# Who issues the loads: compression pages on SyncE alone, pair weights on Pool's queue half a pair ahead

## The chip, the cores and the metric

One core of a Trainium2 chip runs the whole program. The metric is the device time of one execution in microseconds; the median of several runs is compared. Traces are one profiled execution each, and times in them count from its first instruction.

## The reference

One layer of a decoder for a prompt of 1024 rows and 8 samples of 4 new rows each, 1056 rows in all, everything float32. What the change touches:

```
h = RMSNorm(x) * (1 + scale1) + shift1
z = h @ w_in          # columns: gMLP u|v, q, k/v of three branches, branch gates, merge gates
...
kv_rows = past rows from cache_kv[page_table] (8192 per sample) + the new ones
kc, vc  = compress_blocks(kv_rows)    # each 64-row block: gelu(einsum(block + pe, w1) + b1) @ w2 + b2
o_cmp, o_sel, o_win = attention over compressed blocks, over the top 16 blocks, over a window of 512
```

The compression reads the compressed-branch half of every page of all eight samples. Those pages are 64 MB of the traffic.

## The kernel before, in words

Products run with weights and activations split into two float32r parts each (hi and lo, three matmuls per product). `split` and `parts_into` make such parts: a cast on ScalarE (L332, L822) and a subtraction on VectorE (L333, L823).

The instructions are given to a scheduler, which makes an order for each engine in advance from the order of the program and from the times that it reckons with; on the chip each engine runs its own list strictly in order. A wait at the head of a list holds up all that stands behind it, and that goes for SyncE, ScalarE and Pool as issuers of DMAs too. In the attention stage the order on TensorE is that of the program. The DMAs of SyncE and ScalarE share eight completion semaphores in turn, so a DMA of the two waits until the one eight places before it has landed; Pool's DMAs have eight of their own.

The pages of the compressed branch come in 16 loads of 32 pages of 128 KB, one buffer. `step(n)` runs the compression of load n on TensorE (`compress`, 64 pairs of matmuls that each read all 32 pages), its activation on ScalarE (`compress_act`, L569), and then issues load n + 1 (`compress_load`). `load_pages` (L538) deals the eight groups of four pages out to queues: groups whose place modulo eight is in `share` go to ScalarE's queue, here (1, 4), the rest to SyncE's. Before each group the queue's engine reads four entries of the page table (L528).

The stages up to the attention: row products for keys and values (steps 1, 2), the gMLP stage (steps 3, 4), and then the pair stage. It computes columns of z two blocks at a time in 11 pairs (queries 2, merge gates 8, keys 1) with a scheme that saves one of eight quarter products. `pair` loads four raw weight tiles of 256 KB, a11, a12, a21, a22, into a ring of four buffers. It needs weight sums made on Pool, s1 = a21 + a22 and s2 = s1 - a11, later s3 = a11 - a21 (over a21) and s4 = a12 - s2 (over a12), and sums of parts of h (T2, T3, T4 and the changed B12). A quarter product is 12 matmuls of 304 columns; a11, a12, a21 and a22 are used on the remaining 448 columns as well. The order of weights in an ordinary pair is a11, a12, s2, a21, s3, s1, a22, s4. There are three buffers each for hi and lo parts, so a split can run up to three weights ahead of TensorE.

The sums of h are made once, in the opening pair: `sums_of(k)` for T2, T3 and T4, then `last_sums` for B12, on Pool, VectorE and ScalarE. The temporary `e` of `sums_of` lives in the tiles that later hold s1 and s2, so these come after the sums. `pair` is a generator; between its parts the loop runs `step(5)` to `step(14)`.

The attention follows. It has four page buffers (`page_buffer`), which hold window rows (w_k, w_v), selected pages (`psel`) and weights w_ada in turn. The first use of each buffer makes Pool copy one element of the loaded queries into its first element (L1064), so that what is loaded there waits for the queries.

Of the kernel before, what the change touches and what calls it, by code (L numbers as in the profile page):

```python
# [6 lines left out]
F32 = mybir.dt.float32  # L7
# [4 lines left out]
OP = mybir.AluOpType  # L12
# [7 lines left out]
HQ = 304  # L20
# [33 lines left out]
def step_kernel(tc, A):  # L54
    nc = tc.nc
    sync, act, dve, pool, pe = nc.sync, nc.scalar, nc.vector, nc.gpsimd, nc.tensor
# [19 lines left out]
    def new_pool(name, side=None):  # L76
        kw = {} if side is None else {"side": side}
        return TP(tc.alloc_tile_pool(name=name, bufs=1, reuse_waits="tile", **kw))
# [95 lines left out]
    for gr in range(2):  # L174
        e = tmpi([128, 32])
# [4 lines left out]
    for b in range(8):  # L180
        e = tmpi([128, 32], F32, "e", 2)
# [22 lines left out]
    e = tmpi([128, 32])  # L204
# [3 lines left out]
    W = new_pool("weights", "right")  # L208
# [121 lines left out]
    def split(t, hi, lo):  # L330

        act.copy(hi, t)  # L332
        dve.tensor_tensor(lo, t, hi.bitcast(F32), op=OP.subtract)  # L333
# [212 lines left out]
    def compress_load(n):  # L546
        b, half = n // 2, n % 2
        home = "a"
        st = PG([128, 32, 256], F32, "st", 1)
        load_pages([(st[:, i], A["pcmp"], b * 64 + half * 32 + i) for i in range(32)], freed.get(home),  # L550
                   (1, 4))
        paged[n] = st, home

    def compress(n):
# [120 lines left out]
    for tt in range(9):  # L675
        n = 128 if tt < 8 else 32
        st = RV2([128, 6], F32, "bn", 2)[0:n]
# [5 lines left out]
    for tt in range(9):  # L683
        n = 128 if tt < 8 else 32
# [43 lines left out]
    W = new_pool("weights2", "right")  # L728
# [85 lines left out]
    def out_tile():  # L814
        homes[0] += 1
        return TR([128, R], F32, "o", 1) if homes[0] % 3 == 0 else slot()

    def sum_tile(i):
        return TR([128, 512], F32, f"sum{i}", 1)

    def parts_into(x, hi, lo):
        act.copy(hi, x)  # L822
        dve.tensor_tensor(lo, x, hi.bitcast(F32), op=OP.subtract)  # L823

    def sums_of(k):

        (h11, l11), (h12, l12), (h21, l21), (h22, l22) = (f32(x[k]) for x in (B11, B12, B21, B22))
        t = TR([128, R], F32, "o", 1)
        f0, f1, d = (t[:, HQ * i:HQ * i + HQ] for i in range(3))
        e = sum_tile(k % 2)[:, 0:HQ]  # L830
        pool.tensor_tensor(d, l22, l12, op=OP.subtract)
        dve.tensor_tensor(f0, h22, h12, op=OP.subtract)
        dve.tensor_tensor(f0, f0, d, op=OP.add)
        dve.tensor_tensor(f1, f0, h11, op=OP.add)
        dve.tensor_tensor(f1, f1, l11, op=OP.add)
        parts_into(f1, *T2[k])
        pool.tensor_tensor(e, h21, f1, op=OP.subtract)
        pool.tensor_tensor(e, e, l21, op=OP.add)
        parts_into(f0, *T3[k])
        parts_into(e, *T4[k])  # L840
# [12 lines left out]
    def weight_parts(x):  # L853
        hi, lo = (W([128, 512], F32R, tag, 3) for tag in ("hi", "lo"))
        split(x, hi, lo)
        return [[t[:, c:c + 128] for c in range(0, 512, 128)] for t in (hi, lo)]
# [8 lines left out]

    rest = [tuple(t[:, 2 * HQ:R] for t in (hh[k], hl[k])) for k in range(8)]

    def pair(m, n, ev, opening=False, closing=False):

        raws = []  # L870
        for j, c in ((m, 0), (m, 512), (n, 0), (n, 512)):
            raws.append(W([128, 512], F32, "raw", 4))
            act.dma_start(raws[-1], A["w_t"][j][:, c:c + 512])
        a11, a12, a21, a22 = raws
        g, t = out_tile(), out_tile()
        first, second, third = slice(0, HQ), slice(HQ, 2 * HQ), slice(2 * HQ, R)
        plain = [pA()[:, 0:R - 2 * HQ] for _ in range(2)]
        X, S, Z = pA()[:, 0:HQ], pT()[:, 0:HQ], pT()[:, 0:HQ]
        add = lambda o, x, y: dve.tensor_tensor(o, x, y, op=OP.add)  # L879
        s1, s2 = sum_tile(0), sum_tile(1)  # L880

        w = weight_parts(a11)
        quarter_products(w, rest[0:4], plain[0], True, False)
        quarter_products(w, B11, X, True, True)
        act.copy(g[:, first], X)
        w = weight_parts(a12)
        quarter_products(w, rest[4:8], plain[0], False, True)
        quarter_products(w, B21, X, False, True)
        ev(t[:, third], plain[0])
        ev(t[:, first], X)  # L890
        yield
        pool.tensor_tensor(s1, a21, a22, op=OP.add)  # L892
        pool.tensor_tensor(s2, s1, a11, op=OP.subtract)
        if opening or closing:
            quarter_products(weight_parts(a21), rest[0:4], plain[1], True, False)
        if opening:
            quarter_products(weight_parts(a22), rest[4:8], plain[1], False, True)
            ev(g[:, third], plain[1])
            yield
        if not (opening or closing):  # L900
            quarter_products(weight_parts(s2), T2, S, True, True)
            add(t[:, second], S, g[:, first])
            quarter_products(weight_parts(a21), rest[0:4], plain[1], True, False)
        s3, s4 = a21, a12
        pool.tensor_tensor(s3, a11, a21, op=OP.subtract)
        pool.tensor_tensor(s4, a12, s2, op=OP.subtract)
        if closing:
            w = weight_parts(a22)
            quarter_products(w, rest[4:8], plain[1], False, True)
            ev(g[:, third], plain[1])  # L910
            Y = pA()[:, 0:HQ]
            quarter_products(w, T4, Y, True, True)
            quarter_products(weight_parts(s1), B12, Z, True, True)
            ev(g[:, second], Z)
            quarter_products(weight_parts(s4), B22, Z, False, True)
            ev(t[:, second], Z)
            w = weight_parts(s2), weight_parts(s3)
            quarter_products(w[0], T2, S, True, True)
            for o in (t, g):
                add(o[:, second], g[:, first], o[:, second])  # L920
            add(t[:, second], S, t[:, second])
            quarter_products(w[1], T3, S, False, True)
            add(g[:, first], Y, g[:, first])
            add(g[:, second], S, g[:, second])
            add(g[:, first], S, g[:, first])
            yield t, g
            return
        if opening:
            quarter_products(weight_parts(s2), T2, S, True, True)
            add(t[:, second], S, g[:, first])  # L930
        quarter_products(weight_parts(s3), T3, S, False, True)
        add(g[:, second], S, g[:, first])
        quarter_products(weight_parts(s1), B12, Z, True, True)
        add(g[:, second], Z, g[:, second])
        w = weight_parts(a22)
        quarter_products(w, T4, S, False, True)
        add(g[:, first], S, g[:, first])
        ev(g[:, 0:2 * HQ], g[:, 0:2 * HQ])
        if not opening:
            quarter_products(w, rest[4:8], plain[1], False, True)  # L940
            ev(g[:, third], plain[1])
        quarter_products(weight_parts(s4), B22, Z, False, True)
        add(t[:, second], Z, t[:, second])
        ev(t[:, second], t[:, second])
        yield t, g
# [29 lines left out]
                pool.dma_start(A["o_wsk"][b][:, 508:512], kr[:, NP + 4 * b:NP + 4 * b + 4])  # L975

    n = 5
    for i in range(11):
        j = 2 * i
        m, fn, ev, base = ((4 + j, query, scaled, 4) if i < 2 else (6 + j, merge_gate, gate, 10) if i < 10 else  # L980
                           (8, key, lambda o, x: act.copy(o, x), 8))
        work = pair(m, m + 1, ev, i == 0) if i < 10 else pair(9, 8, ev, False, True)
        next(work)
        if i == 0:
            for k in range(4):
                sums_of(k)
            next(work)
            last_sums()
        if i < 10:
            step(n)  # L990
            n += 1
        out = next(work)
        for x, j in zip(out, (m - base, m + 1 - base)) if i < 10 else zip(out[::-1], range(2)):
            fn(j, x)
        if i in (5, 6, 7, 8):
            next(first_blocks, None)
    for b in range(8):
# [44 lines left out]
    qt = [slot() for _ in range(4)]  # L1042
# [14 lines left out]
    def page_buffer():  # L1057

        n = len(uses)
        uses.append(None)  # L1060
        assert n < 4 or uses[n - 4] is not None
        st = R3S([128, 4, 4, 256], F32, f"st{n % 4}", 1)
        if n < 4:
            pool.tensor_copy(st[0:1, 0, 0, 0:1], qt[3][0:1, 0:1])  # L1064
        return n, st, uses[n - 4] if n >= 4 else None

    YS = R3([128, 8, 32])
# [373 lines left out]
    begin, m = None, 0  # L1441
# [124 lines left out]
    W = new_pool("weights3", "right")  # L1566
# [30 lines left out]
    for m in range(8):  # L1597
        t = slot()
# [56 lines left out]
    for a, b in CH:  # L1655
        acc = None
        for m in range(8):
            products(weights(A["w_out"][m], 8), mh, ml, a, b,
                     lambda a, b, ps, m=m: residual(x1[m], m, gate1, a, b, ps, x1[m]),
# [433 lines left out]
```

## Time and profile before

| what | value |
|---|---|
| median of 3 runs | 1952.53 us (1951.09 to 1954.44) |
| the profiled execution | 1954.05 us, span 1952.5 us |
| TensorE matmul busy | 1843.3 us, 94% of the span |
| TensorE weight load busy | 1707.8 us, 87% |
| VectorE, ScalarE, Pool busy | 1247.9, 837.7, 612.7 us |
| mean granted TensorE clock | 0.983 |
| HBM traffic | 178 GB/s over the span |

How to read it: PE is TensorE's matmuls and PEld its weight loads. DVE is VectorE, ACT ScalarE, POOL Pool (GpSimd) and SP SyncE; a q behind an engine's name means its sequencer, which waits and issues DMAs and isn't counted as busy. A row of the timeline gives start, duration, engine, line, operation, tiles, count, and in brackets the idle time before it with what ended it. Matmuls are pipelined and their ends are modelled.

### The profile page before, as it was taken

To read this page: it belongs to the slowest core of one execution; us is meant where nothing else is said; L and a number is where in the kernel's file an instruction comes from. 1 tells how busy PE (TensorE), PEld (TensorE's weight loads), DVE (VectorE), ACT (ScalarE), POOL (GpSimd) and SP (SyncE) were. 2 spreads that over 40 slices of the span, in tenths; PEclk is the share of its full clock that TensorE was granted. 3 is DMA by queue.
4 is the path that set the end of the run, shared out by engine and by line. 5 is a ranking of instruction groups with operands and counts; after the bars stand their busy time and mean duration, and the time that the engine had idled before them with its cause. 6 is when DMAs were issued, how large, how long until landed. Compare 5 with 4: busy or idle time off the path is not lost.

```text
span 1952.5 us, 43825 instructions
## 1 busy us (share of the span) xinstructions
PE 1843.3 (94%) x15905; PEld 1707.8 (87%) x15905; DVE 1247.9 (64%) x2547; ACT 837.7 (43%) x1707; POOL 612.7 (31%) x809
## 2 busy tenths in 40 slices
PE   5999969999998799999999999999999999999997
PEld 3999968989888577776779999899999999999997
DVE  7525264243426576776664768999988888756464
ACT  4413022222224464656661355644444444555343
POOL 2410242121213122222210511387766765301010
PEclk9999989999999899999999999999999999999999
DMA  9545446565655797887753555233322223677464
GB/s 330 186 143 169 158 152 207 167 214 182 221 190 178 229 282 241 272 265 231 236 187 122 214 167 179 71 105 121 110 82 85 78 82 99 220 243 227 124 194 114
DMA packets 241848, 345.35 MB, mean 177 GB/s; under 512 B 35265, under 2 KB 173409, under 8 KB 239457
## 3 DMA queue, kind: packets, MB, share of 16 engines
q1 hardware_dynamic: 194416, 249.99, 40.6%
q0 software_dynamic: 17808, 58.16, 8.5%
q10 hardware_dynamic: 29408, 34.40, 5.6%
q8 instruction: 126, 2.06, 0.4%
q14 instruction: 90, 0.73, 0.1%
HBM read 305.17 MB, written 41.43 MB: 178 GB/s over the span
## 4 chain that ended last, share of the span: by engine, by line
PE 74%; DVE 8%; DMA 6%; issue 4%; ACT 4%; POOL 2%; SPq 1%; ACTq 0%; DVEq 0%; POOLq 0%
PE t L63 70%; PE t L67 3%; DMA t<-pcmp 2%; DVE t L333 2%; DMA t<-t 1%; ACT t L332 1%; DVE t L1725 1%; DMA t<-psel 1%; DMA t<-o_rows 1%; DMA t<-w_up 1%; DVE t L1726 0%; ACT t L1305 0%; DVE t L823 0%; ACT t L1334 0%; POOL t L1751 0%
## 5 line engine op out<-in xcount | busy, mean ns | idle before, releaser
L63 PE MATMUL t<-t,t 128*128 128x264 f32 (+12 forms) x15130 | 1768.0, 306 | 94.3 <-ACT t L332 30.9
L63 PEld LDWEIGHTS t<-t,t 128*128 128x128 f32 (+2 forms) x14970 | 1625.7, 169 | 176.9 <-issue 59.7
L332 ACT CAST t<-t 128x512 fp32r<-128x512 f32 (+5 forms) x589 | 336.9, 592 | 522.9 <-PE t L63 312.3
L333 DVE TENSOR_TENSOR t<-t,t 128x512 fp32r<-128x512 f32 (+5 forms) x523 | 432.6, 838 | 181.4 <-ACT t L332 174.2
L67 PEld LDWEIGHTS t<-t,t 128*128 128x128 f32 x746 | 81.6, 144 | 33.1 <-issue 9.0
L1773 DVE TENSOR_TENSOR t<-t,t 128x264 f32<-128x264 f32 (+2 forms) x296 | 92.3, 345 | 27.9 <-PE t L63 25.7
L67 PE MATMUL t<-t,t 128*128 128x128 f32 x746 | 107.0, 279 | 3.0 <-ACT t L1372 1.5
L879 DVE TENSOR_TENSOR t<-t,t 128x304 f32<-128x304 f32 x55 | 25.8, 472 | 115.7 <-PE t L63 112.2
L538 POOL DMA_DIRECT2D t<-psel x128 | 70.7, 553 | 77.4 <-DMA t<-psel 38.2
L892 POOL TENSOR_TENSOR t<-t,t 128x512 f32<-128x512 f32 x11 | 15.7, 1426 | 229.3 <-DMA t<-w_t 190.1
L1927 POOL TENSOR_TENSOR t<-t,t 128x384 f32<-128x384 f32 (+1 forms) x12 | 14.0, 1198 | 223.6 <-ACT t L1994 223.6
L1304 DVE TENSOR_REDUCE t<-t 128x1 f32<-128x640 f32 (+3 forms) x64 | 58.7, 920 | 34.1 <-PE t L63 33.8
L1334 ACT COPY t<-t 128x512 f32<-128x512 f32 (+1 forms) x112 | 59.8, 569 | 36.3 <-PE t L67 35.9
L1726 DVE SCALAR_TENSOR_TENSOR t<-t,t,t 128x1072 f32<-128x1072 f32 x44 | 73.4, 1669 | 0.0
L1724 ACT ACTIVATE t<-t,t 128x1072 f32<-128x1072 f32 x44 | 56.6, 1287 | 37.1 <-DVE t L1773 24.3
L1725 DVE SCALAR_TENSOR_TENSOR t<-t,t,t 128x1072 f32<-128x1072 f32 x44 | 70.2, 1596 | 3.3 <-ACT t L1724 3.2
L1305 ACT ACTIVATE t<-t,t 128x640 f32<-128x640 f32 (+3 forms) x64 | 56.2, 880 | 25.0 <-DVE t L1304 22.5
L1830 POOL TENSOR_TENSOR t<-t,t 128x1024 f32<-128x1024 f32 x22 | 54.6, 2480 | 20.5 <-ACT t L1829 20.5
L1361 POOL COPY t<-t 128x256 f32<-128x256 f32 x32 | 12.9, 403 | 133.0 <-DVE t L1359 62.8
L721 POOL TENSOR_TENSOR t<-t,t 128x512 f32<-128x512 f32 (+1 forms) x12 | 11.5, 970 | 131.4 <-issue 112.2
L1604 POOL TENSOR_TENSOR t<-t,t 128x384 f32<-128x384 f32 (+1 forms) x24 | 27.9, 1166 | 66.4 <-DVE t L1603 63.3
L1720 POOL COPY t<-t 128x2 f32<-128x2 f32 x44 | 33.2, 754 | 49.1 <-DVE t L1773 49.1
(294 smaller groups left out, 1385.2 us busy)
## 6 DMA issues: line engine op xcount, KB each, us to landing
t<-pcmp SPq DMA_DIRECT2D x384, 128.0 KB
t<-psel SPq DMA_DIRECT2D x384, 128.0 KB
t<-w_down SPq DMA_DIRECT2D x120, 256.0 KB
t<-t POOLq DMA_DIRECT2D x54, 528.0 KB, 3.3
t<-w_up SPq DMA_DIRECT2D x96, 256.0 KB
t<-pcmp ACTq DMA_DIRECT2D x128, 128.0 KB
t<-psel POOLq DMA_DIRECT2D x128, 128.0 KB, 4.0
t<-w_ada SPq DMA_DIRECT2D x16, 1024.0 KB
```

Source lines behind the costliest of these rows:

```text
L63: return pe.matmul(out, lhsT, rhs, start=start, stop=stop, skip_group_check=skip)
L67: return pe.transpose(out, x, ident)
L332: act.copy(hi, t)
L333: dve.tensor_tensor(lo, t, hi.bitcast(F32), op=OP.subtract)
L538: d = queue.dma_start(dst, src[bass.ds(r, 1)].rearrange("g p c -> p (g c)"))
L1304: dve.tensor_reduce(m4[:, branch, h:h + 1], ps[:, :, 0:w], axis=AX.XY, op=OP.max, negate=True)
L1305: act.activation(P[:, 0:L].rearrange("p (a c) -> p a c", a=2), ps[:, :, 0:w], AF.Exp, bias=m4[:, branch, h:h + 1], accum_out=s4[:, branch, ...
L1334: (act.copy if w > 2 else dve.tensor_copy)(probs[branch, h][:, 128 * k:128 * (k + w)], pt[:, c:c + 128 * w])
L1724: act.activation(acc[:, 0:w], up[:, 0:w], AF.Identity, scale=cw[:, n, 0:1], bias=cw[:, n, 3:4])
L1725: dve.scalar_tensor_tensor(acc[:, 0:w], up[:, 1:1 + w], cw[:, n, 1:2], acc[:, 0:w], op0=OP.mult, op1=OP.add)
L1726: dve.scalar_tensor_tensor(acc[:, 0:w], up[:, 2:2 + w], cw[:, n, 2:3], acc[:, 0:w], op0=OP.mult, op1=OP.add)
L1773: dve.tensor_tensor(o, by4(banks[c][:, c0:c0 + n], n), other(c, c0, n), op=OP.add)
```

## The change

Four edits. (1) Loads 4 to 15 of the compressed pages are issued by SyncE alone; loads 0 to 3 deal three groups of eight to ScalarE instead of two. (2) The raw weights of a pair are loaded on Pool's queue, by a new `pair_load` that is called half a pair ahead (behind s3 and s4 of the pair before) and in the order a11, a21, a22, a12. (3) s1 and s2 are computed at the beginning of a pair. In the opening pair the temporary `e` lives in the second part of the pair's two output tiles, which the generator now yields, so s1 and s2 no longer wait for the sums of h. (4) The copies of L1064 are gone: loads into the four page buffers no longer wait for the queries.

```diff
     def compress_load(n):
...
         load_pages([(st[:, i], A["pcmp"], b * 64 + half * 32 + i) for i in range(32)], freed.get(home),
-                   (1, 4))
+                   (1, 4, 6) if n < 4 else ())
...
-    def sums_of(k):
+    def sums_of(k, e):
...
-        e = sum_tile(k % 2)[:, 0:HQ]
...
-    def pair(m, n, ev, opening=False, closing=False):
-
+    def pair_load(m, n):
         raws = []
-        for j, c in ((m, 0), (m, 512), (n, 0), (n, 512)):
+        for j, c in ((m, 0), (n, 0), (n, 512), (m, 512)):
             raws.append(W([128, 512], F32, "raw", 4))
-            act.dma_start(raws[-1], A["w_t"][j][:, c:c + 512])
-        a11, a12, a21, a22 = raws
+            pool.dma_start(raws[-1], A["w_t"][j][:, c:c + 512])
+        return raws
+
+    def pair(raws, ev, opening=False, closing=False):
+
+        a11, a21, a22, a12 = raws
...
+        pool.tensor_tensor(s1, a21, a22, op=OP.add)
+        pool.tensor_tensor(s2, s1, a11, op=OP.subtract)
         w = weight_parts(a11)
...
-        yield
-        pool.tensor_tensor(s1, a21, a22, op=OP.add)
-        pool.tensor_tensor(s2, s1, a11, op=OP.subtract)
+        yield t, g
...
         pool.tensor_tensor(s4, a12, s2, op=OP.subtract)
+        yield
...
+    PAIR = [(4, 5), (6, 7)] + [(10 + 2 * i, 11 + 2 * i) for i in range(8)] + [(9, 8)]
+    raws = pair_load(*PAIR[0])
     for i in range(11):
...
-        next(work)
+        work = pair(raws, ev, i == 0, i == 10)
+        tiles = next(work)
         if i == 0:
             for k in range(4):
-                sums_of(k)
+                sums_of(k, tiles[k % 2][:, HQ:2 * HQ])
             next(work)
             last_sums()
         if i < 10:
             step(n)
             n += 1
+        next(work)
+        if i < 10:
+            raws = pair_load(*PAIR[i + 1])
         out = next(work)
...
         st = R3S([128, 4, 4, 256], F32, f"st{n % 4}", 1)
-        if n < 4:
-            pool.tensor_copy(st[0:1, 0, 0, 0:1], qt[3][0:1, 0:1])
         return n, st, uses[n - 4] if n >= 4 else None
```

More of the change, by code (lines that the diff above doesn't have):

```diff
@@ L977, in step_kernel @@
     n = 5
+    PAIR = [(4, 5), (6, 7)] + [(10 + 2 * i, 11 + 2 * i) for i in range(8)] + [(9, 8)]
+    raws = pair_load(*PAIR[0])
     for i in range(11):
[L979 to L982, printed above, removed]
-        next(work)
+        fn, ev, base = ((query, scaled, 4) if i < 2 else (merge_gate, gate, 10) if i < 10 else
+                        (key, lambda o, x: act.copy(o, x), 8))
+        work = pair(raws, ev, i == 0, i == 10)
+        tiles = next(work)
         if i == 0:
             for k in range(4):
-                sums_of(k)
+                sums_of(k, tiles[k % 2][:, HQ:2 * HQ])
             next(work)
@@ L991, in step_kernel @@
             n += 1
+        next(work)
+        if i < 10:
+            raws = pair_load(*PAIR[i + 1])
         out = next(work)
-        for x, j in zip(out, (m - base, m + 1 - base)) if i < 10 else zip(out[::-1], range(2)):
-            fn(j, x)
+        for x, j in sorted(zip(out, PAIR[i]), key=lambda p: p[1]):
+            fn(j - base, x)
         if i in (5, 6, 7, 8):
```

## The prediction

> **What bounds the kernel now.** I read the page first (busy shares, the chain that ended last), then the chain in order of time, then TensorE's waits and tables by stretch around the places that the diff touches.
>
> ```profile
> span 1952.5 us, 43825 instructions
> PE 1843.3 (94%) x15905; PEld 1707.8 (87%) x15905; DVE 1247.9 (64%) x2547; ACT 837.7 (43%) x1707; POOL 612.7 (31%) x809
> PE 74%; DVE 8%; DMA 6%; issue 4%; ACT 4%; POOL 2%; SPq 1%; ACTq 0%; DVEq 0%; POOLq 0%
> 69.40 182.24 PE t L63 x1850
> ```
>
> TensorE is the bound (94% busy, 74% of the chain). The change adds and removes no product, so it can win only where TensorE stands still or runs at a low clock. Up to 251.6 us it does neither: one unbroken piece of 182 us. The diff acts behind that, in the pair stage (254 to 626 us) and at its end. In the tables the columns are: stretch, length, then PE, PEld, DVE, ACT and POOL busy with counts, granted clock, DMA share, GB/s.
>
> ```profile
> 256.70:260.00 3.30, 3.25 (x10) 2.98 (x11) 3.27 (x5) 1.24 (x2) 1.40 (x2) 0.58 1.05 381
> 287.00:293.50 6.50, 0.00 (x0) 0.00 (x0) 4.24 (x7) 1.95 (x5) 2.40 (x3) 0.50 0.34 96
> 293.60:297.00 3.40, 3.40 (x13) 3.18 (x14) 1.84 (x3) 0.97 (x3) 0.00 (x0) 0.50 0.90 253
> 329.40:585.80 256.40, 247.14 (x2202) 229.85 (x2202) 93.54 (x158) 67.25 (x126) 54.02 (x48) 0.99 0.61 199
> 626.00:648.20 22.20, 8.04 (x40) 5.50 (x41) 13.00 (x32) 10.87 (x20) 3.55 (x11) 0.57 1.05 366
> PE t L63 <- ACT t L332: 10.8, 8, 2.0
> ```
>
> In the eight periods from 329.4 to 585.8 TensorE loses 10.8 us to weight casts on ScalarE (L332), and one more wait of 0.5 on VectorE: 11.3 us over nine loads of pages, 1.26 each. The larger holes are at both ends of the stage, and a hole costs twice: the clock is 0.50 to 0.58 just behind it.
>
> **The change part by part.**
>
> *Pages off ScalarE (loads 4 to 15).* One period, from the release of the page buffer at 418.94:
>
> ```profile
> 418.94 0.49 ACT L569 ACTIVATE t<-t,t 128x128 f32<-128x128 f32 x1 [6.11 <-PE t L63]
> 419.67 6.14 ACTq L538 DMA_DIRECT2D t<-pcmp  x8
> 425.85 1.66 ACT L332 CAST t<-t 128x512 fp32r<-128x512 f32 x3 [6.42 <-DMA t<-pcmp]
> 426.52 3.72 PE L63 MATMUL t<-t,t 128*128 128x304 f32 x15 [1.62 <-ACT t L332]
> 427.04 15.22 PEld L63 LDWEIGHTS t<-t,t 128*128 128x128 f32 x82 [0.22 <-ACT t L332]
> 442.56 0.81 PEld L63 LDWEIGHTS t<-t,t 128*64 128x64 f32 x18 [0.30 <-issue]
> 452.10 1.97 PEld L63 LDWEIGHTS t<-t,t 128*128 128x128 f32 x14 [0.17 <-issue]
> ```
>
> ScalarE issues eight pages for 6.14 us, part of it waiting for earlier pages to land; the next cast stands behind them, and TensorE idles 1.62. Without them the cast can follow at 419.7, and that idle time goes. What is late next is the pages, since SyncE now issues 32 and not 24:
>
> ```profile
> 418.94 0.33 SPq L538
> 419.46 0.33 SPq L538
> 419.97 3.50 DMA t<-pcmp
> 423.49 2.36 DMA t<-pcmp
> L538 SPq DMA_DIRECT2D t<-pcmp x24: 332/333/333, 418.9 to 435.3; - x24
> L528 SPq TENSOR_LOAD <-t x6: 298/302/303, 420.9 to 435.7; - x6
> SPq L538 <- PE t L63: 12.6, 1, 12.6
> SPq L538 <- DMA t<-pcmp: 4.6, 8, 1.7
> ```
>
> SyncE's step from page to page is 0.52 (418.94 to 419.46); each four pages need a read of the page table, 0.30 plus a gap of 0.04. All 32: 31 x 0.52 + 7 x 0.34 = 18.5 us from first to last issue, against 16.4 now (418.9 to 435.3), when both queues wait for landings. A landing takes 2.4 to 3.5, so the last page is there 20.9 to 22.0 after the release. The compression that reads all 32 starts when TensorE has done its work between: 256.4 us are eight periods of 32.05; less 11.3 / 9 idle that is 30.8 of work; less the compression (442.56 to 452.10, 9.5) it is 21.3. So the pages come between 0.4 early and 0.7 late; the slack of 12.6 that SyncE shows today is spent on issue (2.1) and on landing and the next compression (10). I take a wait of 0.6 in place of 1.26, toward the late end, because SyncE's 4.6 us of waiting for landings won't vanish wholly: 9 x -0.66 = **-6**. Ends: -11.3 (all pages early) and +9 (a wait of 2.3).
> The Trainium skill (DMA: Bandwidth & Descriptors, "Issuing engines are not separate DMA queues") holds that issuing from several engines saves only sequencer time, usually small beside the transfer; by that alone this term would be -11.3. The trace agrees that the two queues share one rate, but here sequencer time is 18.5 of the 21.3 us at hand.
>
> *Load 4*, in the unbroken stretch, has less room:
>
> ```profile
> L538 SPq DMA_DIRECT2D t<-pcmp x24: 332/333/789, 212.1 to 228.8; - x24
> 232.99 0.42 PEld L63 LDWEIGHTS t<-t,t 128*64 128x64 f32 x8 [0.25 <-issue]
> ```
>
> 212.1 + 18.5 + 2.4 to 3.5 = 233.0 to 234.1 against 232.99: **+0.6** (0 to +1.1). Load 5 has 11 us more. In loads 0 to 3 ScalarE gets twelve pages in place of eight, some 2 us more of blocking; TensorE lost nothing to eight in the 182 us above: 0 (to +2).
>
> *Weights on Pool's queue.* ScalarE loses 4 issues a pair, Pool gains 4; Pool is busy 54 of 256 us above, so it has room. Behind a load that waits for its buffer stand Pool's s1 and s2 for the next pair and the stores of gates, none due before the third product of the next pair. The tightest is a12: its buffer comes free with the last cast of a pair (s4), which can be made when s3's product is done; s1, a22, s4 and a11 (12 + 24 + 12 + 24 products, at 15.22 / 82 = 0.186) then give 13.4 us. Cast and subtraction take some 1.5, and pages on Pool's queue land thus:
>
> ```profile
> DMA to landing us min/median/max: 2.6/4.0/7.7
> ```
>
> 1.5 + 7.7 + 1.5 for a12's own split is 10.7: hidden, 0, and s1, s2 come earlier than today. Were the cover gone, each us beyond would cost 10 us in all.
>
> *The opening pair.*
>
> ```profile
> 251.73 1.80 ACTq L873 DMA_DIRECT2D t<-w_t  x4
> 253.47 2.69 POOL L721 TENSOR_TENSOR t<-t,t 128x512 f32<-128x512 f32 x3 [17.57 <-issue]
> 256.75 22.44 PE L63 MATMUL t<-t,t 128*128 128x448 f32 x208 [2.97 <-ACT t L332]
> 280.61 0.72 DVE L823 TENSOR_TENSOR t<-t,t 128x304 fp32r<-128x304 f32 x1 [0.51 <-ACT t L822]
> 283.83 1.43 POOL L893 TENSOR_TENSOR t<-t,t 128x512 f32<-128x512 f32 x1 [0.80 <-DVE t L823]
> 292.00 0.85 ACTq L538 DMA_DIRECT2D t<-pcmp  x2
> 292.89 0.62 ACT L332 CAST t<-t 128x512 fp32r<-128x512 f32 x1 [0.59 <-issue]
> 293.56 6.66 PE L63 MATMUL t<-t,t 128*128 128x304 f32 x30 [14.37 <-ACT t L332]
> ```
>
> First weights: issued at 251.73 behind ScalarE's last activation, they make TensorE wait 2.97, then run at clock 0.58 (3.3 x 0.42 = 1.4 lost). Pool stood idle 17.6 us before 253.47, so in its order the loads can go out long before; then up to -4.4. If they are put behind L721 and its store, at 257, they land some 5 later: +4. Most likely the first go ahead and the last behind: **-2**.
> The h-sums: TensorE waits 14.37 for s2's cast at 292.89, which ScalarE does last, behind the last sums and the pages. The sums that s2's product needs are complete at 281.3 (280.61 + 0.72); s2 itself, now on Pool's list before the sums, no longer waits for their temporaries (283.83 today). So the products of s2, s3 and a22 (36 x 0.186 = 6.7 us) can run before 293, while those that need the last sums can't: VectorE is busy 4.24 of the last 6.5 us, and the casts moved ahead give it 2 us more to do. Up to -6.7 and -2.3 for the clock (0.50 for 3.4 us, less than 1 for some more); nothing but the two pages' 0.85 if the order stays. I take **-5.5** (-9 to -0.9), since no row shows a reason for s2 to be late any more.
>
> *The gate on the page buffers* (L1064):
>
> ```profile
> 641.07 0.53 POOL L1064 COPY t<-t 1x1 f32<-1x1 f32 x4 [0.30 <-DMA t<-o_rows]
> 641.27 0.42 SPq L1221 DMA_DIRECT2D t<-w_ada  x1
> 648.21 3.64 PE L63 MATMUL t<-t,t 128*32 128x512 f32 x16 [7.53 <-DMA t<-w_ada]
> ```
>
> Four copies on Pool wait until the queries are loaded; half of w_ada is issued behind them and TensorE waits 7.53. Ungated it can go out at 624 and land before 640.7. The cover is not free: the DMA engines are full there (share 1.05 at 366 GB/s), so its 1 MB puts 2.8 us on queries and values, which TensorE needs only behind the w_ada products. **-6**; ends: -7.5, and +3 if w_k and pages (2 to 3 MB, 8 us) also pass ahead of queries and values.
>
> *Sum:* -6 + 0.6 + 0 - 2 - 5.5 - 6 = -18.9. The profiled execution took 1954.05 (span 1952.5), the median of the runs is 1952.53, 1.5 less: 1954.05 - 18.9 = 1935.1, as a median **1934**.
>
> **The rivals.** *SyncE becomes the bound* (the slower side). If its 4.6 us of waiting stays on top of 18.5, the last page is there after 25.5 to 26.6, 4.2 to 5.3 behind TensorE: with 4.7 for 1.26, nine loads give +31, so -18.9 + 6 + 31 = +18: 1970. It decides from a wait of 2.7 a load. For it: the waits are there. Against: they arise while ScalarE adds its eight; alone SyncE takes 8 x 0.52 + 0.7 = 4.9 for eight pages, and a landing 3.5.
> *Weights late on Pool's queue.* If landings grew to 13 us, a12 would come 2.6 late in ten pairs: -18.9 + 26 = +7: 1960. Against it: 7.7 is the longest. The Trainium skill (SBUF — State Buffer, "SBUF: two separate sides", on DMAs from GpSimd) warns that these stall while VectorE holds the shared port, about 0.6 us growing to 3.1; by it I estimate 2.5 more for each of four loads, 10 in a row, which would fill the cover; no row here shows such a stall.
> *Only the pairs gain.* The order of ScalarE in the opening stays and queries are delayed as much as w_ada is hastened: -6 + 0.6 - 0.9 = -6: 1946. For it: a list of work written in the same order.
> *All at its better end:* -11.3 - 4.4 - 9 - 7.5 = -32: 1920.
>
> **How the numbers follow.** Forecast 0.55 (1926 to 1942); only the pairs 0.19; better than 1926 0.1; SyncE 0.1; late weights 0.06. The range from 1920 to 1950 leaves out 0.16 above and a little below. No change means within 0.2%, 3.9 us, about what a measurement can tell. Faster: 0.55 + 0.1 + 0.17 of the pairs' case = 0.82; slower: 0.08; the rest 0.1.
>
> **What will show it.** No page issue of step 6 and later on ScalarE, and its cast right behind L569; 32 pages in 18 to 19 us on SyncE and TensorE's wait before the compression (today none) under 1 us; no wait of TensorE over 7 us at the end of the stage; the wait before s2's product under 9, clock behind it above 0.5. Wrong would be: waits for pages of 2 us and more, or casts that wait for w_t.

## The result, and the profile after

The changed kernel takes 1926.7 us (median of 4 runs, 1925.4 to 1935.02) against 1953.49 for the kernel before on the same chip: a ratio of 0.9871, 95% interval 0.9839 to 0.9902. 1934 was forecast with a range of 1920 to 1950, so the forecast held. Its terms did not: they came out right together because several that were too large made up for one that was far too small, and that is luck. The profiled execution took 1926.18 (span 1924.6).

The page of the changed kernel, with busy shares and the chain that ended last:

```profile
span 1924.6 us, 43777 instructions
PE 1828.4 (95%) x15905; PEld 1701.1 (88%) x15905; DVE 1243.1 (65%) x2547; ACT 840.1 (44%) x1707; POOL 636.5 (33%) x849
PE 73%; DVE 8%; DMA 6%; SPq 4%; issue 4%; ACT 3%; POOL 1%; DVEq 0%; ACTq 0%; POOLq 0%
```

The same 15905 matmuls are busy for 14.9 us less (1843.3 before). Of the 27.9 us by which the span is shorter, more than half is thus no idle time saved but products that run faster, and a sum over idle times can't see it. SyncE's sequencer is now 4% of the chain (1% before).

For all kernels below I use three marks that stand for the same work in each: A, the first page issue of load 7; B, the first issue of w_ada, which waits for the last compression to release its pages; C, a group of eight w_ada products behind a hole of 1.77 or 1.78 us that every kernel has (665.94 before, 638.74 after; in act_pages a wait for pages splits the group in two). A depends on the order of TensorE's list and only tells where a difference begins.

| kernel | A | B | C | span | median of the runs |
|---|---|---|---|---|---|
| before | 321.4 | 624.26 | 665.94 | 1952.5 | 1951.7 to 1953.5 in four series |
| after | 316.8 | 607.88 | 638.74 | 1924.6 | 1926.7 |
| gate_back | 317.7 | 606.88 | 640.78 | 1929.2 | 1928.9 |
| only_gate | 321.2 | 624.80 | 656.96 | 1945.0 | 1947.3 |
| act_pages | 317.9 | 622.63 | 651.68 | 1948.3 | 1944.4 |
| act_weights | 322.5 | 615.15 | 641.77 | 1930.1 | 1931.4 |
| only_pages | 322.9 | 616.83 | 643.46 | 1927.7 | 1925.9 |
| late_sums | 315.9 | 604.77 | 635.42 | 1925.9 | 1926.8 |
| one_group | 316.1 | 599.61 | 635.67 | 1925.9 | 1928.1 |
| pool_group | 322.3 | 605.26 | 638.92 | 1927.2 | 1929.9 |
| queries_first | 319.4 | 623.57 | 660.00 | 1946.8 | 1947.6 |
| pages_gate | 321.0 | 615.87 | 639.87 | 1925.6 | 1924.7 |
| pool_two | 318.5 | 605.01 | 646.91 | 1931.7 | 1935.7 |
| one_queries | 316.3 | 599.33 | 631.74 | 1916.2 | 1921.7 |

From before to after 4.6 us are gained by A, 16.4 by B, 27.2 by C and 27.9 over the span. So the gain is made between the opening pair and the first w_ada products, and the rest of the program keeps it.

*The pairs.* TensorE's waits (and those of its weight loads) between 300 and 612 us, the kernel before first and then the changed one:

```profile
PE t L63 <- ACT t L332: 11.4, 9, 2.0
PEld t L63 <- ACT t L332: 16.4, 19, 2.3
```

```profile
PE t L63 <- DMA t<-pcmp: 7.5, 5, 2.2
PE t L63 <- issue: 1.7, 1, 1.7
PEld t L63 <- ACT t L332: 0.2, 1, 0.2
```

Waits for casts (16.4 us in 19 weight loads) are gone but for 0.2, and waits for pages stand in their place. TensorE's own waits fell only from 11.9 to 9.2 us. The 304-column products of the pairs, grouped by shape (busy time, mean of one), before (305 to 600) and after (300.2 to 580.8, nearly the same work):

```profile
L63 PE MATMUL t<-t,t 128*128 128x304 f32 x778 | 127.7, 313 | 11.3 <-ACT t L332 10.8 <-DVE t L800 0.5
```

```profile
L63 PE MATMUL t<-t,t 128*128 128x304 f32 x783 | 117.9, 304 | 0.0
```

They are busy 9.8 us less for five more products. One load's pages, and the pair products between the release of the buffer and the next compression, first before (418.9 to 442.5), then after (415.6 to 440.6):

```profile
L63 PE MATMUL t<-t,t 128*128 128x304 f32 x72 | 13.0, 336 | 1.6 <-ACT t L332 1.6
L63 PE MATMUL t<-t,t 128*128 128x448 f32 x48 | 10.6, 366 | 0.0
```

```profile
L63 PE MATMUL t<-t,t 128*128 128x304 f32 x94 | 14.2, 304 | 0.0
L63 PE MATMUL t<-t,t 128*128 128x448 f32 x52 | 11.4, 366 | 0.0
```

The same load in the timeline of the changed kernel, SyncE's issues and the compression's first matmul, and SyncE's waits from 415 to 441:

```profile
415.56 21.24 SPq L538 DMA_DIRECT2D t<-pcmp  x32
440.71 31.23 PE L63 MATMUL t<-t,t 128*64 128x128 f32 x284 [1.23 <-DMA t<-pcmp]
```

```profile
SPq L538 <- DMA t<-pcmp: 3.2, 3, 2.0
```

SyncE alone needs 21.2 us for the 32 issues, 3.2 of them waiting for landings, and the compression starts 25.15 behind the release. But TensorE's list was made anew with the change and now has 146 pair products there instead of 120 (twelve of the 26 stood inside the compression before), so TensorE waits 1.23.

*The end of the stage.* SyncE's longest wait from 600 to 645 us before, its issues after, and TensorE's holes after:

```profile
SPq L1221 <- PE t L63: 20.6, 1, 20.6
```

```profile
595.32 2.08 SPq L1051 DMA_DIRECT2D t<-t  x4
597.50 1.49 SPq L1054 DMA_DIRECT2D t<-o_rows  x2
607.88 0.82 SPq L1226 DMA_DIRECT2D t<-w_ada  x2
```

```profile
612.75 0.57 PE L63 MATMUL t<-t,t 128*64 128x64 f32 x8 [2.44 <-ACT t L569]
616.56 8.76 PE L63 MATMUL t<-t,t 128*128 128x320 f32 x43 [3.24 <-ACT t L1310]
638.74 1.51 PE L63 MATMUL t<-t,t 128*32 128x512 f32 x8 [1.78 <-issue]
```

Before, the first half of w_ada stood ahead of the queries on SyncE and waited 20.6 us for the last compression; the queries went out behind it at 625.13, the gate opened at 641.07, and TensorE waited 7.53 for the other half. After, the queries are out at 595.32 and no wait for w_ada is left.

### The profile page after: what moved, and what is told of

Same layout as the page of the kernel before. It is cut to its first block, busy times and chain, and to the rows that moved or that the text cites. A ratio compares the mean times of both kernels' runs of the same rounds, so it can differ in the third digit from the quotient of the medians.

```text
span 1924.6 us, 43777 instructions
## 1 busy us (share of the span) xinstructions
PE 1828.4 (95%) x15905; PEld 1701.1 (88%) x15905; DVE 1243.1 (65%) x2547; ACT 840.1 (44%) x1707; POOL 636.5 (33%) x849
## 4 chain that ended last, share of the span: by engine, by line
PE 73%; DVE 8%; DMA 6%; SPq 4%; issue 4%; ACT 3%; POOL 1%; DVEq 0%; ACTq 0%; POOLq 0%
PE t L63 70%; SPq L538 4%; PE t L67 3%; DVE t L333 2%; DMA t<-pcmp 1%; DMA t<-w_ada 1%; DMA t<-t 1%; DMA t<-psel 1%; ACT t L332 1%; DVE t L1730 1%; DVE t L1853 1%; SPq L528 1%; ACT t L1310 0%; DMA t<-w_t 0%; ACT t L1339 0%
## 5 line engine op out<-in xcount | busy, mean ns | idle before, releaser
L871 POOL DMA_DIRECT2D t<-w_t x44 | 24.6, 559 | 93.9 <-DVE t L333 76.9
L569 ACT ACTIVATE t<-t,t 128x128 f32<-128x128 f32 x16 | 7.9, 493 | 99.4 <-PE t L63 99.4
L1609 POOL TENSOR_TENSOR t<-t,t 128x384 f32<-128x384 f32 (+1 forms) x24 | 27.9, 1167 | 64.6 <-DVE t L1608 61.4
```

## The experiments

**Undoing one edit, doing one alone.** *gate_back*, the changed kernel with

```diff
+        if n < 4:
+            pool.tensor_copy(st[0:1, 0, 0, 0:1], qt[3][0:1, 0:1])
```

> The changed kernel with the four copies of L1064 put back, so that what goes first into the four page buffers of the attention waits for the queries again. Theory: the gate's removal is worth 10 to 11 us, the 7.5 us wait for w_ada and the clock behind the holes (23.9 us at half clock before, 10.2 after), so this runs at 1936 to 1938 and shows again a wait for w_ada of some 7 us and low clock of over 20 us at the end of the pair stage. Rival: the gate itself was worth the 6 us that the prediction gave it or less, and the rest of the gain at the end came with the pages or the weights: 1930 to 1933, with a shorter wait for w_ada.

1928.9 (1923.29 to 1930.81), ratio to before 0.9876 (0.9838 to 0.9914). That is below both ranges and on the rival's side: the gate put back costs some 2 us, within the spread of the runs. TensorE's wait:

```profile
623.84 3.54 PE L63 MATMUL t<-t,t 128*32 128x512 f32 x16 [2.30 <-DMA t<-w_ada]
```

The queries are out early, so the gate opens at 612.3 and the wait is 2.30, not 7.

*only_gate*, the kernel before without those two lines.

> The kernel before with the four copies of L1064 taken away and nothing else. If the gains add up by place, it runs at 1953 - 10.5 = 1942 to 1943, and the stretches of the pair stage ahead of 620 us are as before. If the end's gain needs that SyncE, and no longer ScalarE, issues the last pages: 1946 to 1948. Rival with a loss: the queries and values come later for the w_ada that passes them, 1953 or more.

1947.28 (ten runs), ratio 0.998 (0.9962 to 0.9998), in the second of the three ranges: a gain of 4.4 us, and 9.0 at mark C of the profiled run, of which 7.5 are left at the end. SyncE's issues and TensorE's first long hole:

```profile
624.80 0.83 SPq L1219 DMA_DIRECT2D t<-w_ada  x2
625.67 3.15 SPq L1044 DMA_DIRECT2D t<-t  x4
633.58 2.18 PE L63 MATMUL t<-t,t 128*128 128x320 f32 x7 [4.55 <-ACT t L1303]
```

Both halves of w_ada go out at once and the wait for them is gone; the queries stay late and the hole of 4.55 ahead of it stays too. Alone the gate costs 4 to 9 us; with the other edits in place it costs about 2. These gains don't add.

*act_pages*, the changed kernel with

```diff
-                   (1, 4, 6) if n < 4 else ())
+                   (1, 4))
```

> The changed kernel with two groups of eight of every load of pages on ScalarE's queue again (share 1 and 4), the other three edits kept. Theory: the pair stage's 12 us come from the pages, since ScalarE's issue of eight pages stands ahead of the casts; the kernel then runs at 1936 to 1939, with waits of TensorE for casts of 1 to 2 us a pair as before. Rival: they come from the weights that left ScalarE's queue and from the earlier s1 and s2; then this is 1927 to 1930 with hardly a wait for casts. Third: SyncE alone is the slower of the two (waits for pages of 1 to 2 us a load in the changed kernel), and this is faster, 1918 to 1924.

1944.41 (ten runs), ratio 0.9962 (0.9944 to 0.998): 17.7 slower than the changed kernel, more than the theory's 10 to 12, so its time is a miss. The waits for casts between 300 and 612 us are back whole, though the weights are on Pool's queue and s1 and s2 early:

```profile
PE t L63 <- ACT t L332: 11.4, 9, 2.1
PEld t L63 <- ACT t L332: 15.7, 18, 2.3
```

*act_weights*, the changed kernel with the weights issued by ScalarE, still half a pair ahead:

```diff
-            pool.dma_start(raws[-1], A["w_t"][j][:, c:c + 512])
+            act.dma_start(raws[-1], A["w_t"][j][:, c:c + 512])
```

> The changed kernel with the pair weights issued by ScalarE, still half a pair ahead and with pages on SyncE alone. Theory: four issues of a weight tile cost ScalarE about 0.5 us each, ahead of no cast that is due, so 1927 to 1930. Rival: ScalarE's list waits for the release of a buffer or for landings in the queue's semaphores that it shares with SyncE's 32 pages, its casts come late, and the pair stage loses 1 us or more a pair: 1937 to 1945.

1931.44, ratio 0.9897 (0.9862 to 0.9933), between the two expectations. No cast comes late; the loss has another place:

```profile
604.88 13.18 PE L63 MATMUL t<-t,t 128*64 128x128 f32 x162 [13.12 <-DMA t<-pcmp]
```

TensorE's list has as many pair products between two compressions as the changed kernel (91 and 56 in the period from 418.9), but for the last load, released at 581.73, only 51 are left where the changed kernel has 118 (from 574.64). They run out before the pages are there, and TensorE waits 13.12.

*only_pages*, the kernel before with the page edit alone:

```diff
-                   (1, 4))
+                   (1, 4, 6) if n < 4 else ())
```

> The kernel before with one edit: pages from load 4 on issued by SyncE alone (and three groups instead of two on ScalarE in loads 0 to 3). The changed kernel without this edit ran at 1944.4, so with the others in place it is worth some 17 us. Theory: nearly all of the gain is this edit's, in the pairs and at the end of the stage, which it brings forward; then this is 1933 to 1938, and its wait for w_ada is under 4 us though the copies of L1064 are there. Rival: it needs the weights on Pool's queue half a pair ahead, since here four weight loads of a pair are still issued on ScalarE's queue when their buffers come free: then 1942 to 1950.

1925.92 (1922.55 to 1929.31), ratio 0.9862 (0.9848 to 0.9876): the whole gain of the change, with the gate, the weights on ScalarE's queue and s1, s2 late. Faster than the theory's 1933 to 1938. SyncE's issues and TensorE's longest waits:

```profile
604.19 1.87 SPq L1044 DMA_DIRECT2D t<-t  x4
616.83 1.25 SPq L1221 DMA_DIRECT2D t<-w_ada  x2
606.51 13.22 PE L63 MATMUL t<-t,t 128*64 128x128 f32 x162 [9.49 <-DMA t<-pcmp]
621.68 8.35 PE L63 MATMUL t<-t,t 128*128 128x320 f32 x43 [1.95 <-ACT t L1305]
```

With the page edit the queries come ahead of w_ada in SyncE's list, so the gate has nothing to hold up. The pages of the last load are waited for 9.49 us, and the kernel is as fast nevertheless.

*late_sums*, the changed kernel with s1 and s2 moved back behind the first part of a pair.

```diff
-        pool.tensor_tensor(s1, a21, a22, op=OP.add)
-        pool.tensor_tensor(s2, s1, a11, op=OP.subtract)
         w = weight_parts(a11)
...
         yield t, g
+        pool.tensor_tensor(s1, a21, a22, op=OP.add)
+        pool.tensor_tensor(s2, s1, a11, op=OP.subtract)
```

> The changed kernel with s1 and s2 put back behind the first part of a pair (the temporaries stay in the output tiles). Theory: in the opening the sums of h on VectorE are the bound and not s2, so their place is worth 0 to 2 us there and nothing in the other pairs: 1926 to 1930. Rival, the prediction's step: s2's early place frees the products behind it, and its loss costs 5 us: 1931 to 1934, with a wait of over 8 us before s2's product.

1926.78, ratio 0.9864 (0.9847 to 0.9882): no difference, as the theory has it. TensorE's waits from 270 to 300 us are 10.3 us there (6.4 + 1.8 + 1.5 + 0.4 + 0.2) and 9.8 in the changed kernel, whose rows are:

```profile
PE t L63 <- ACT t L822: 5.6, 3, 3.6
PE t L63 <- DVE t L881: 1.8, 2, 1.6
PE t L63 <- DVE t L333: 1.8, 1, 1.8
PE t L63 <- DVE t L823: 0.4, 1, 0.4
PE t L63 <- ACT t L332: 0.2, 1, 0.2
```

**Is SyncE alone too slow?** *one_group*: one group of four pages back on ScalarE.

```diff
-                   (1, 4, 6) if n < 4 else ())
+                   (1, 4, 6) if n < 4 else (1,))
```

> The changed kernel with one of the eight groups of four pages of loads 4 to 15 on ScalarE's queue (share 1) in place of none. Theory: SyncE alone is now the bound of the pairs by a little (20 to 21 us from first to last issue, TensorE waits 0.95 to 2.16 us for pages in seven of the loads); with 28 pages it is done 2.5 us earlier, those waits go, and the 3 us of issue on ScalarE fit ahead of the cast that is due: 1917 to 1923. Rival: four issues in front of the casts already make TensorE wait, and the clock drops behind the holes: 1928 to 1938.

1928.14, ratio 0.9881 (0.9866 to 0.9895): no gain, so the theory's time is a miss. The waits went most of the way that it expected: 2.6 us for pages between 300 and 590 (7.5 in the changed kernel up to 612), 0.2 for casts. Mark B is 8 us earlier, and most of it is lost behind it, where one half of w_ada again stands ahead of the queries:

```profile
599.61 0.35 SPq L1226 DMA_DIRECT2D t<-w_ada  x1
600.01 4.18 SPq L1051 DMA_DIRECT2D t<-t  x4
608.62 7.75 PE L63 MATMUL t<-t,t 128*128 128x320 f32 x35 [5.06 <-ACT t L1310]
619.62 1.94 PE L63 MATMUL t<-t,t 128*32 128x512 f32 x8 [3.25 <-DMA t<-w_ada]
```

*pool_group*: that group on Pool's queue instead (a third choice of `share` in `load_pages`).

```diff
+            own = (2 if n == 12 else 0) if share == "pool" else (2 if n == 4 else 0) if share == "third" else int(len(starts) % 8 in share)
...
-                   (1, 4, 6) if n < 4 else ())
+                   (1, 4, 6) if n < 4 else "third")
```

> The changed kernel with one of the eight groups of four pages of loads 4 to 15 on Pool's queue. Theory: as with one group on ScalarE's queue the waits for pages go, and Pool, which has s1 to s4 and four weight loads a pair, has time for four more: 1916 to 1922. Rival: Pool waits at the head of its list for the release of the page buffer, the weights and sums behind it come late, and TensorE waits for these: 1930 to 1945.

1929.93, ratio 0.9888 (0.987 to 0.9905), a miss of the theory again. Waits for pages are 1.7 us from 250 to 590, but the opening lost 4.0 to a DMA and 6.2 to a cast in one piece, and w_ada stands ahead of the queries (605.26 and 606.13).

**What of the page edit is worth what?** *queries_first*, the kernel before with w_ada and wv kept behind the queries on SyncE:

```diff
-        sync.dma_start(VV[i][:, 0:1024].rearrange("p (k c) -> p k c", c=256),
+        vv = sync.dma_start(VV[i][:, 0:1024].rearrange("p (k c) -> p k c", c=256),
...
+            with tc.issue_after(vv.ins) if use < 4 else ExitStack():
                 sync.dma_start(st[:, p0:p0 + 2048], A["w_ada"][ch][:, p0:p0 + 2048])
```

> The kernel before with one change of order: on SyncE the first w_ada and wv are issued behind the queries and the o_rows, not ahead of them. The gate of L1064 and the pages on ScalarE stay. Theory: the 7.5 us wait for w_ada has two causes in a row, w_ada waits on SyncE for the last compression and holds up the queries, and the gate then waits for these; so either remedy takes it away, and this gains what the gate's removal alone did, 4 to 8 us: 1944 to 1948, queries issued by 605 and no wait for w_ada over 3 us. Rival: the queries wait for something else until 625 and nothing changes: 1950 to 1953.

1947.58 (ten runs), ratio 0.9977 (0.9958 to 0.9997): 4.7 us, as the removed gate alone, so either remedy takes the same wait away. The queries went at 614.40 (not by 605: they waited 12.2 us for TensorE), and the wait for w_ada is 1.39.

*pages_gate*: both edits in the kernel before, the page edit and the removed gate.

> The kernel before with the page edit and without the gate; the weights stay on ScalarE's queue and s1, s2 in their old place. Theory: with the page edit the queries are ahead of w_ada on SyncE anyway, so the gate is worth nothing more: 1924 to 1928, like the page edit alone (1925.9). Rival: the two edits add, 1925.9 - 4.4 = 1921 or less.

1924.73 (1923.82 to 1927.19), ratio 0.9859 (0.9836 to 0.9882). Beside the page edit the gate's removal is worth 1.2 us, inside the spread. This kernel also lacks the edits to weights and sums, and it is not slower than the changed one.

*pool_two*, the kernel before with ScalarE's two groups of loads 4 to 15 on Pool's queue; SyncE keeps 24 pages.

```diff
+            own = (2 if n == 12 else 0) if share == "pool" else (2 if n in (4, 16) else 0) if share == "two" else int(len(starts) % 8 in share)
...
-                   (1, 4))
+                   (1, 4) if n < 4 else "two")
```

> The kernel before with the eight pages of loads 4 to 15 that ScalarE issued put on Pool's queue; SyncE keeps its 24. Theory: what costs is that ScalarE's casts stand behind its page issues; with ScalarE free the casts' waits go as with the page edit, the page chain is shorter than SyncE's alone, and 1924 to 1932 results (the end of the stage may still have its wait for w_ada). Rival: the gain comes from the order of TensorE's products that goes with 32 pages on SyncE (about 146 pair products between two compressions and none inside one, where it was 132 with twelve of them inside): then this stays at 1940 to 1950.

1935.72 (1933.24 to 1938.95), ratio 0.9922 (0.9898 to 0.9946). From load 7 on TensorE's list has 120 pair products between two compressions and twelve inside one, as before, so the rival (TensorE's order) is out for this part: only ScalarE was freed. The time is some 4 us above the theory's range, which goes with the end of the stage. Its 304-column products between one release and the next compression (409.1 to 429.3, the 72 that took 13.0 us before); then the stretch from A to B, in the kernel before and in this one (start, end and length, PE and its count, PEld, DVE, ACT, POOL, granted clock, DMA share, GB/s); then the timeline at the end of the stage:

```profile
L63 PE MATMUL t<-t,t 128*128 128x304 f32 x72 | 10.8, 304 | 0.0
```

```profile
321.40:624.20 302.80, 291.51 (x2554) 270.82 (x2554) 115.30 (x194) 82.77 (x157) 67.20 (x65) 0.99 0.59 191
318.50:605.00 286.50, 284.87 (x2554) 267.65 (x2554) 109.11 (x194) 84.96 (x157) 105.32 (x138) 1.00 0.61 202
```

```profile
605.01 0.35 SPq L1221 DMA_DIRECT2D t<-w_ada  x1
605.89 3.10 SPq L1044 DMA_DIRECT2D t<-t  x4
613.81 2.18 PE L63 MATMUL t<-t,t 128*128 128x320 f32 x7 [4.55 <-ACT t L1305]
629.00 3.64 PE L63 MATMUL t<-t,t 128*32 128x512 f32 x16 [7.57 <-DMA t<-w_ada]
```

From A to B it takes 286.5 us where the kernel before took 302.8: 16.3 us in the pairs for the same 2554 products. TensorE's idle time falls by 9.7 of them (11.3 to 1.6), its busy time by 6.6. At the end everything is as before: w_ada ahead of the queries, holes of 4.55 and 7.57. There this kernel loses what it had gained over the page edit alone: it is 11.8 us ahead of only_pages at B and 3.5 behind at C.

*one_queries*, one group on ScalarE with the queries first on SyncE (one_group and the `issue_after` of queries_first, also for wk).

> The changed kernel with one group of four pages on ScalarE's queue from load 4 on, and on SyncE the first w_ada, wk and wv behind the queries and o_rows. One group alone left a wait of 3.25 us for w_ada and one of 5.06 us ahead of it. Theory: with the queries first the 3.25 goes, and 1922 to 1925 results, a little below the changed kernel. Rival: the end of the stage is bound by the loads themselves (DMA engines full), and it stays at 1926 to 1929.

1921.68 (five runs, 1917.83 to 1929.68), ratio 0.9856 (0.9831 to 0.9881): the fastest of all. The wait for w_ada is 0.47, mark C 7.0 us ahead of the changed kernel (the profiled run is the fastest of the five). Its interval overlaps that of the changed kernel's ratio, so it surely beats the kernel before and only probably the changed one.

```profile
594.82 2.12 SPq L1051 DMA_DIRECT2D t<-t  x4
599.33 5.55 SPq L1229 DMA_DIRECT2D t<-w_ada  x2
617.26 1.07 PE L63 MATMUL t<-t,t 128*32 128x512 f32 x8 [0.47 <-DMA t<-w_ada]
```

## Why the prediction was right, and where its steps were wrong

*Pages off ScalarE: -6 forecast, -26 measured alone* (1951.71 to 1925.92). It has two parts. The first is shown: ScalarE freed is worth 16 us in the pairs (pool_two). The second, 10 between the medians of pool_two and only_pages and 4 between their profiled runs, is shown in part. only_pages comes to B 11.8 us behind pool_two, since its last pages are late, but from B to C it takes 26.6 us instead of 41.9. Of these 15.3 the wait for w_ada was 7.57, and what removes that wait alone gains 4.4 to 4.7 in the medians (only_gate, queries_first). The rest is read from the traces alone: one hole of 1.95 stands where there were holes of 4.55 and 1.26, and the granted clock between B and C is 0.87 instead of 0.71. TensorE's list is another one too in only_pages, and no run separates the two.

The mechanism in the pairs was the one forecast, casts behind page issues; the size was wrong for three reasons. First, the sum counted visible idle time, 11.3 us, and took only 6 of it. The products around it were slow as well: the same 2554 are busy 6.6 us less in pool_two, and that is time a list of idle pieces doesn't show. The clock (last section) explains some 2 of the 6.6, by estimate: at half clock 15 products took 3.3 us once and 3.4 us once, and at the 0.151 us of the changed kernel (94 in 14.2) they would have taken 2.3. For the other 4 or so there is a hint that no run tests: between A and B of the kernel before the weight loads waited 15.6 us for casts, 4.8 more than the matmuls did.

Second, I charged SyncE's lateness to TensorE. The arrival was forecast 20.9 to 22.0 us behind the release; it took 25.15, nearly the 25.5 to 26.6 of the rival "SyncE becomes the bound". From first to last issue SyncE took 19.5 to 22.1 us in the loads from 240 us on, not the 18 to 19 that the prediction looked for, and one wait for pages passed its mark for being wrong, 2 us. That rival's price, 4.7 a load, didn't follow, since the 21.3 us of work between two compressions were taken as fixed while the scheduler put 26 more products there; TensorE waits 1.23 in this load. The lateness comes due at the end of the pairs: the last pages are waited for 2.16 us in the changed kernel, 9.49 in only_pages, 13.12 in act_weights.

Third, a new time for the pages moves other entries of SyncE's list. The queries went ahead of w_ada, and no step of the prediction looked at that.

The Trainium skill's rule (DMA: Bandwidth & Descriptors, "Issuing engines are not separate DMA queues"), that several issuers save only a little sequencer time, would have given -11.3 for this term, nearer the 16 us of the pairs than -6. Its reason is not borne out: 21.2 us of issue are most of the 25.15 between release and compression, but TensorE had other work for them.

*Load 4: +0.6 forecast, nothing seen.* TensorE's first holes from 200 us on, in the timeline of the changed kernel:

```profile
253.98 4.55 PE L63 MATMUL t<-t,t 128*128 128x448 f32 x24 [0.70 <-DVE t L333]
260.34 1.90 PE L63 MATMUL t<-t,t 128*128 128x448 f32 x8 [1.82 <-DVE t L333]
```

*Weights on Pool's queue: 0 forecast, 0 measured.* In the changed kernel TensorE has no wait for w_t, and pages_gate, which lacks this edit, runs at 1924.7. The stall of DMAs from GpSimd that the Trainium skill warns of (SBUF — State Buffer, "SBUF: two separate sides") would have shown as late weights. The trace of the changed kernel shows none: its 44 loads landed after 2.9 to 5.2 us. With four pages more on that queue (pool_group) TensorE waited 1.2 us for w_t; whether such a stall was the reason, no run shows.

*The opening: -2 and -5.5 forecast.* The first weights did as forecast (one issued at 235.34, three at 250.41; TensorE waits 0.70 and 1.82, the two rows above, instead of 2.97, and the clock behind them is 1.00 instead of 0.58). In the h-sums the waits fell from 14.4 to 9.8, but not for the reason given: with s1 and s2 late they are 10.3. The low clock didn't go either: it is 0.50 from 279.6 to 289.8 us. only_pages has 7.0 us of holes there (5.70, 0.17, 0.85, 0.29) with neither of these edits. The failed step is "no row shows a reason for s2 to be late any more": that s2's own list of work was shorter did not show that TensorE would be released by it. Beside the page edit the opening's edits are worth nothing that can be measured.

*The gate: -6 forecast, -4.4 alone (interval -0.4 to -7.4), about -2 in the changed kernel.* The wait for w_ada was read rightly, and it is gone. But it had two causes in a row, the queries' place behind w_ada on SyncE and the gate behind the queries; the page edit removes the first, and then the gate's removal finds little left.

So -18.9 was forecast and -26.8 measured, nearly all of it in one term, which was sized at -6; the other terms, sized as if each stood alone, had shares of the same gain counted a second time. What stays open: what the products of the pairs lose beyond the clock in the kernel before, how the gain between B and C divides between the order of SyncE's list and that of TensorE's, why act_pages loses 10 us of its gain behind mark C in its profile (the slowest of its ten runs), and the spread of 2 to 14 us between runs of one kernel.

## What to carry to other kernels

A late cast costs more than the idle time in front of TensorE: compare the busy time of the same products, and ask what the whole stretch would take without the stall. Before adding terms, ask of each pair of edits whether they remove the same wait; here one edit had the whole gain, and the run that does it alone shows that more quickly than undoing the others. When a list is planned anew, look for what else has changed places in it: the queries moved past a DMA that waited 20.6 us, by an edit to other loads.

## What the runs showed of the hardware that was not expected

The granted clock fell to 0.50 for one stretch of some 3.4 us behind holes of only 1.62 and 1.78 us (at 426.52 and 361.28 in the kernel before), but not behind 1.68 (at 394.61) or 2.05 (329.42). Rows of the kernel before; the clock is the third value from the end:

```profile
427.90:431.20 3.30, 3.30 (x15) 3.30 (x14) 1.16 (x3) 0.62 (x1) 0.00 (x0) 0.50 0.90 280
363.10:366.50 3.40, 3.40 (x15) 3.40 (x14) 1.15 (x3) 0.62 (x1) 0.00 (x0) 0.50 0.87 254
394.40:397.70 3.30, 3.09 (x19) 2.83 (x20) 2.06 (x4) 1.51 (x4) 0.00 (x0) 1.00 0.87 251
```

Fifteen products in place of some 20 fit into such a stretch, and it counts as busy. The Trainium skill (TensorE: Matmul & The Clock Gate, "Part 1: The HAM clock gate") puts the drop behind an idle window of about 3.4 us; in these rows holes of half that length were enough in two cases of four.
